# A head's exponentials move behind the first piece of projection work on ScalarE

## The chip, the cores and the metric

One core of a Trainium2 chip. The metric is the device time of one execution in microseconds (us); three runs of the kernel before gave 1851.01, 1851.04 and 1851.13.

## The reference, cut to what matters

Two layers on 256 tokens of width 2048, float32. Layer 0 mixes the tokens with a convolution module, layer 1 with the attention below, and behind each stands a squared-ReLU MLP.

```python
def mla(h, cos, sin, w_in, q_norm_g, kv_norm_g, w_q_up, w_kv_up, w_o):
    down = h @ w_in
    c_q, c_kv, k_pe = jnp.split(down, [512, 1024], axis=-1)
    q = (rms_norm(c_q, q_norm_g) @ w_q_up)        # 16 heads of 128 + 64
    kv = (rms_norm(c_kv, kv_norm_g) @ w_kv_up)    # 16 heads of 128 (k) + 128 (v)
    ...
    s = (q_nope . k_nope + rope(q_pe) . rope(k_pe)) * scale, masked by chunks of 64
    p = softmax(s)
    return (p @ v) @ w_o
```

## The kernel before

Every matmul in full precision is made of three in a rounded format: a value is split into an upper part `hi` and a lower part `lo`, and three products of the parts are summed. For weights the split is made on the fly: ScalarE (ACT) rounds the loaded tile `raw` into `hi` (L174) and VectorE (DVE) subtracts to get `lo` (L175). Results in PSUM that feed another such product are split in the same way (ACT at L224, DVE at L229).

The attention of layer 1 runs 16 heads in 4 groups of 4. The order on each engine is that of the code, since the whole part is written under a manual schedule. Each engine works through its own queue in order and waits at an instruction until its inputs are there. In turn of the loop (L1722 to L1748) for a head `h` stand:

1. `scores(h)`: ten matmuls on TensorE (PE) into one PSUM bank, for the two halves of the queries (128 and 256 keys); DVE takes the maximum of each row (L1582) and scales it by -SCALE (L1583); ACT makes the two exponentials (L1585), which also sum their rows, into `pr`.
2. `piece`: a piece of the work of a later group. It is 12 matmuls of the projections of q or kv (`qp_piece`, `qn_piece`, `kv_piece`), with a copy on ACT or DVE behind them, or from head 12 on 12 wider matmuls of the output projection (`o_piece`), with none. Some pieces also put a delayed copy to `qhl` on ACT (`qp_parts`, L1531), which reads a rotation that GpSimd (POOL) has made at L1322 to L1327.
3. `prefetch(1)`: the split of one half of a weight tile, so one `hi` on ACT and one `lo` on DVE, and behind the second half of a tile the load of another on SP's queue.
4. A second piece.
5. `weights_turn(h - 1)`: PE transposes the previous head's weights `pr` (three transposes, L1601), and ACT copies them to `pT` (L1603).
6. In some heads `qp_turn`: four transposes (L1539) and two copies on ACT (L1548, L1549).
7. `values(h - 2)`: three matmuls (L1610, L1611), split into `oh` and `ol`.
8. `weights(h)`: DVE takes the reciprocal of the sums (L1592) and scales `pr` (L1595). This is what step 5 of the next head waits for.
9. Another split, and up to two more pieces, each with a split.

PSUM has 8 banks for all of this. From head 12 on four of them hold the output projection. The `raw` tiles have 3 buffers, `hi` and `lo` 6 each.

Of the kernel before, what the change touches and what calls it, by code (L numbers as in the profile page):

```python
# [87 lines left out]
def trunk_kernel(  # L88
# [55 lines left out]
    def nm(s):  # L144
        uid[0] += 1
        return f"{s}_{uid[0]}"


    def acc_tile():
        return psum["acc"].tile([P, NB], F32, tag="acc", name=nm("acc"))  # L150
# [56 lines left out]
    def mm3_as_is(ps, sh, sl, mh, ml, start, stop):  # L207

        nc.tensor.matmul(ps, sh, mh, start=start, stop=False)  # L209
        nc.tensor.matmul(ps, sl, mh, start=False, stop=False)  # L210
        nc.tensor.matmul(ps, sh, ml, start=False, stop=stop)  # L211
# [1098 lines left out]
    with ExitStack() as cx:  # L1310
# [61 lines left out]
        def u_load(n):  # L1372
            if n < len(units):
                srcs, shape = units[n]
                raw = raws[n] = wpool.tile(shape, F32, tag="raw", name=nm("raw"), bufs=3)
                for i, src in enumerate(srcs):
                    dst = raw if len(srcs) == 1 else raw[:, i : i + 1, :]
                    if len(src.shape) == 4:
                        dst = dst.rearrange("p j (h n) -> p j h n", h=src.shape[2])
                    nc.sync.dma_start(dst, src)  # L1380

        def u_split(n, h):
            if n < len(units):
                parts[n, h] = split_half(raws[n], h, nc.vector)
# [14 lines left out]
        def prefetch(n=9):  # L1399
            while pending and n > 0:  # L1400
                n -= 1
                u, h = pending.pop(0)
                u_split(u, h)
                if h == 1:
                    u_load(u + 3)
# [114 lines left out]
        def piece(work):  # L1520

            due = list(later)
            work()
            for e in due:
                e[0] -= 1
                if e[0] == 0:
                    later.remove(e)
                    e[1]()
# [5 lines left out]
        def qp_turn(g, m):  # L1534

            pt = tr_tile()
            for i in range(2):
                for t in range(T):
                    nc.tensor.transpose(  # L1539
                        pt[:, i * S + t * P : i * S + (t + 1) * P],  # L1540
                        qps[g, t][:, 2 * m + i, :, :].rearrange("p a b -> p (a b)").bitcast(F32),
                        ident,
                    )
            if m == 0:
                qpAs[g] = gp[0].tile([P, HG, S], F32R, tag="qpA", name=nm("qpA"))
            hs = slice(2 * m, 2 * m + 2)
            o = pt.rearrange("p (i n) -> p i n", i=2)
            nc.scalar.activation(qpAs[g][:, hs, :], o, AF.Copy)  # L1548
            nc.scalar.activation(qpB[g % 2][:DR, hs, :], o[:DR], AF.Copy)  # L1549
# [9 lines left out]
        def group_work(g):  # L1559
            kv = kv_work(g)  # L1560
            return q_work(g) + kv


        sides = [(0, 0, P), (1, P, S)]
        scs, prs, zss, pTs = {}, {}, {}, {}

        def scores(h):

            g, i = divmod(h, HG)
            ss = scs[h] = acc_tile()  # L1570
            mx = at2.tile([P, T], F32, tag="mx", name=nm("mx"))
            zs = zss[h] = at2.tile([P, T], F32, tag="zs", name=nm("zs"))
            pr = prs[h] = at2.tile([P, 3 * P], F32, tag="pr", name=nm("pr"))
            for t, at_, n in sides:
                o = ss[:, at_ : at_ + n]
                ts = slice(t * P, (t + 1) * P)
                qT, kT = ([a[:, i, :] for a in x] for x in (qTs[g], kTs[g]))
                mm3_as_is(o, qT[0][:, ts], qT[1][:, ts], kT[0][:, :n], kT[1][:, :n], True, False)
                nc.tensor.matmul(o, qpAs[g][:, i, ts], kpA[:, :n], start=False, stop=False)
                nc.tensor.matmul(o, qpB[g % 2][:, i, ts], kpB[:, :n], start=False, stop=True)  # L1580
            for t, at_, n in sides:
                nc.vector.tensor_reduce(mx[:, t : t + 1], ss[:, at_ : at_ + n], axis=AX.X, op=ALU.max)  # L1582
            nc.vector.tensor_scalar(mx, mx, scalar1=-SCALE, scalar2=None, op0=ALU.mult)  # L1583
            for t, at_, n in sides:
                nc.scalar.activation(  # L1585
                    pr[:, at_ : at_ + n], ss[:, at_ : at_ + n], AF.Exp, bias=mx[:, t : t + 1], scale=SCALE,
                    accum_out=zs[:, t : t + 1],
                )

        def weights(h):  # L1590
            pr, zs = prs[h], zss.pop(h)
            nc.vector.reciprocal(zs, zs)  # L1592
            for t, at_, n in sides:
                q = pr[:, at_ : at_ + n]
                nc.vector.tensor_scalar(q, q, scalar1=zs[:, t : t + 1], scalar2=None, op0=ALU.mult)  # L1595

        def weights_turn(h):
            pr = prs.pop(h)
            pt = tr_tile()
            for b in range(3):  # L1600
                nc.tensor.transpose(pt[:, b * P : (b + 1) * P], pr[:, b * P : (b + 1) * P], ident)  # L1601
            pT = pTs[h] = gp[0].tile([P, 3 * P], F32, tag="pT", name=nm("pT"))
            nc.scalar.activation(pT, pt[:, : 3 * P], AF.Copy)  # L1603

        def values(h):
            g, i = divmod(h, HG)
            pT = pTs.pop(h)
            vs = slice(i * DV, (i + 1) * DV)
            o = acc_tile()[:, :S]
            nc.tensor.matmul(o, vvs[g][:, 0, vs], pT[:, :S], start=True, stop=False)  # L1610
            nc.tensor.matmul(o[:, P:], vvs[g][:, 1, vs], pT[:, S:], start=False, stop=True)  # L1611
            hi_part(o, oh[:, h, :])
            lo_part(o, oh[:, h, :], ol[:, h, :])
# [6 lines left out]
        def o_piece(k):  # L1620
            m, j = divmod(k, 2)
            if k == 0:
                ps_o.extend([[acc_tile() for _ in range(T)] for _ in range(2)])
            start_unit(("o", m), j)
            wh, wl = w_at(("o", m), j)
            for b in range(2):
                bs = slice(b * NB, (b + 1) * NB)
                for t in range(T):
                    mm3(ps_o[b][t], oh_kt(k, t), ol_kt(k, t), wh[:, bs], wl[:, bs], k == 0, k == H - 1)

        with tc.manual_schedule():
# [90 lines left out]
            for g in range(NG):  # L1722
                for i in range(HG):
                    h = g * HG + i

                    n = -(-len(work) // (HG - i))
                    todo, work = work[:n], work[n:]
                    scores(h)
                    piece(todo.pop(0))
                    prefetch(1)  # L1730
                    piece(todo.pop(0))


                    if h > 0:
                        weights_turn(h - 1)
                    if i > 1 and g + 1 < NG:
                        qp_turn(g + 1, i - 2)
                    if h > 1:
                        values(h - 2)
                    weights(h)  # L1740
                    prefetch(1)
                    for w in todo:
                        piece(w)
                        prefetch(1)
                if g + 2 < NG:
                    work = group_work(g + 2)
                elif g + 2 == NG:
                    work = [lambda k=k: o_piece(k) for k in range(H - HG)]  # L1748
# [94 lines left out]
```

## Time and profile before

| | |
|---|---|
| median of 3 runs | 1851.04 us |
| the profiled execution | 1850.8 us |
| its span | 1849.0 us |
| mean granted TensorE clock | 0.998 |
| HBM traffic over the span | 198 GB/s |
| heads, by the first scores and the last values | about 1023 to 1150 us |

The span is the part of an execution in which the profile has instructions; 1.8 us lie around it. Lines are those of the kernel before. A row of the timeline has its start, its duration, the engine, the line, the operation, output and input tiles with their shapes, and how often it stands in sequence; a bracket tells how long the engine was idle before it and what ended that. PEld is the loading of TensorE's stationary operand, which overlaps matmuls.

### The profile page before, as it was taken

What the parts mean: (1) busy time and instruction counts of PE and PEld (TensorE: products, weight loads), DVE (VectorE), ACT (ScalarE), POOL (GpSimd) and SP (SyncE); (2) the same over time, 40 slices, a digit from 0 to 9 for tenths busy, and PEclk for the clock granted to TensorE, in tenths of its full rate; (3) what the DMA queues carried; (4) which work ended last, traced back from release to release, by engine and by line L of the source; (5) the groups of instructions that cost most, each with busy time, mean ns of one, the idle gap of its engine ahead of it and who ended that gap; (6) DMA issues with size and microseconds to landing.
All of it is one profiled execution on the core that took longest, in us unless ns stands there. A gap on an engine that the chain in (4) does not pass through costs nothing.

```text
span 1849.0 us, 28519 instructions
## 1 busy us (share of the span) xinstructions
PE 1816.2 (98%) x10768; PEld 1655.3 (90%) x10768; DVE 1635.4 (88%) x2370; ACT 1205.5 (65%) x1716; POOL 222.6 (12%) x185
## 2 busy tenths in 40 slices
PE   7999999999999999999999999999999999999998
PEld 6999888988988989898899998899898898899886
DVE  5999975789999999999977675667999999999987
ACT  5556663767667677676566665566766766767654
POOL 5999500000000000000001420000000000000000
PEclk9999999999999999999999999999999999999999
DMA  8766366857667666766546445765766766677673
GB/s 236 198 189 185 123 217 182 217 168 226 201 210 230 196 215 223 227 208 218 204 158 196 125 138 197 208 189 170 217 205 211 231 205 204 219 212 220 212 244 114
DMA packets 407113, 367.62 MB, mean 199 GB/s; under 512 B 15416, under 2 KB 351936, under 8 KB 406720
## 3 DMA queue, kind: packets, MB, share of 16 engines
q1 hardware_dynamic: 405952, 363.63, 64.6%
q10 hardware_dynamic: 1024, 2.17, 0.3%
q8 instruction: 84, 1.38, 0.3%
q14 instruction: 53, 0.43, 0.1%
HBM read 363.68 MB, written 2.10 MB: 198 GB/s over the span
## 4 chain that ended last, share of the span: by engine, by line
PE 81%; DVE 14%; ACT 3%; issue 1%; DMA 1%; POOL 0%; DVEq 0%; ACTq 0%
PE acc L539 23%; PE acc L210 14%; PE acc L209 14%; PE acc L211 14%; PE acc L535 12%; DVE sum L1002 8%; DVE lo L175 1%; DVE lo L444 1%; PE acc L274 1%; ACT hi L174 1%; PE acc L219 0%; PE acc L218 0%; PE acc L220 0%; ACT pr L1585 0%; DMA xs<-in_x 0%
## 5 line engine op out<-in xcount | busy, mean ns | idle before, releaser
L444 DVE TENSOR_TENSOR lo<-raw,hi 128x1024 fp32r<-128x1024 f32 (+1 forms) x512 | 571.3, 1125 | 48.6 <-ACT hi L443 48.4
L443 ACT ACTIVATE hi<-raw 128x1024 fp32r<-128x1024 f32 (+1 forms) x512 | 477.2, 968 | 66.5 <-PE acc L210 62.6
L539 PE MATMUL acc<-xt,hi 128*128 128x512 f32 x2048 | 478.5, 380 | 1.7 <-ACT U L547 1.2
L539 PEld LDWEIGHTS acc<-xt,hi 128*128 128x128 f32 x2048 | 377.8, 190 | 49.8 <-ACT U L547 2.0
L209 PE MATMUL acc<-hi,sh 128*128 128x512 f32 x930 | 353.9, 381 | 0.0
L211 PE MATMUL acc<-lo,sh 128*128 128x512 f32 x930 | 353.0, 380 | 0.0
L210 PE MATMUL acc<-hi,sl 128*128 128x512 f32 x802 | 304.4, 380 | 0.0
L535 PEld LDWEIGHTS acc<-xt,lo 128*128 128x128 f32 x2048 | 249.2, 192 | 7.8 <-DVE lo L444 1.0
L535 PE MATMUL acc<-xt,lo 128*128 128x256 f32 x2048 | 250.5, 276 | 0.4 <-DVE lo L444 0.3
L174 ACT ACTIVATE hi<-raw 128x1024 fp32r<-128x1024 f32 (+2 forms) x184 | 179.6, 1004 | 42.5 <-PE acc L210 39.4
L211 PEld LDWEIGHTS acc<-lo,sh 128*128 128x128 f32 x930 | 176.2, 189 | 24.6
L209 PEld LDWEIGHTS acc<-hi,sh 128*128 128x128 f32 x930 | 176.2, 189 | 24.1
L175 DVE TENSOR_TENSOR lo<-raw,hi 128x1024 fp32r<-128x1024 f32 (+2 forms) x118 | 132.8, 1145 | 62.7 <-ACT hi L174 62.4
L210 PEld LDWEIGHTS acc<-hi,sl 128*128 128x128 f32 x802 | 151.9, 189 | 21.1
L1002 DVE SCALAR_TENSOR_TENSOR sum<-ub,w_dw,sum 128x256 f32<-128x256 f32 x392 | 159.5, 498 | 6.0 <-ACT sum L958 5.0
L443 ACT ACTIVATE hi<-V 128x1024 fp32r<-128x1024 f32 x94 | 99.8, 1062 | 96.2 <-DVE V L749 91.6
L175 POOL TENSOR_TENSOR lo<-raw,hi 128x1024 fp32r<-128x1024 f32 x66 | 156.6, 2385 | 22.7 <-ACT hi L174 20.6
L547 ACT ACTIVATE U<-acc 128x512 f32<-128x512 f32 x128 | 75.6, 591 | 127.5 <-PE acc L539 113.4
L218 PE MATMUL acc<-xt,hi 128*128 128x256 f32 x512 | 142.5, 278 | 0.0
L219 PE MATMUL acc<-xt,hi 128*128 128x256 f32 x512 | 141.2, 276 | 0.7 <-DVE xt L231 0.7
L443 ACT ACTIVATE hi<-T 128x1024 fp32r<-128x1024 f32 x94 | 99.1, 1055 | 65.0 <-DVE T L739 60.6
L220 PE MATMUL acc<-xt,lo 128*128 128x256 f32 x512 | 141.2, 276 | 0.0
(275 smaller groups left out, 2803.3 us busy)
## 6 DMA issues: line engine op xcount, KB each, us to landing
raw<-in_mlp_w SPq DMA_DIRECT2D x256, 1024.0 KB, 6.5
raw<-in_conv_w_pw SPq DMA_DIRECT2D x64, 512.0 KB, 5.6
raw<-in_conv_w_pw SPq DMA_DIRECT2D x16, 1024.0 KB, 5.1
raw<-in_mla_w_o SPq DMA_DIRECT2D x16, 1024.0 KB, 5.6
raw<-in_mla_w_kv_up SPq DMA_DIRECT2D x8, 1024.0 KB, 5.4
raw<-in_mla_w_in SPq DMA_DIRECT2D x8, 576.0 KB, 3.9
raw<-in_mla_w_in SPq DMA_DIRECT2D x4, 1024.0 KB, 6.8
raw<-in_mla_w_q_up SPq DMA_DIRECT2D x16, 256.0 KB, 4.4
```

Of the source, the lines that this page charges most:

```text
L174: nc.scalar.activation(hi, raw[:, js, :], AF.Copy)
L175: eng.tensor_tensor(lo, raw[:, js, :], hi.bitcast(F32), op=ALU.subtract)
L209: nc.tensor.matmul(ps, sh, mh, start=start, stop=False)
L210: nc.tensor.matmul(ps, sl, mh, start=False, stop=False)
L211: nc.tensor.matmul(ps, sh, ml, start=False, stop=stop)
L218: nc.tensor.matmul(ps, wh, alternate(th), start=start, stop=False)
L219: nc.tensor.matmul(ps, wh, alternate(tl), start=False, stop=False)
L443: nc.scalar.activation(parts[0], src, AF.Copy)
L444: nc.vector.tensor_tensor(parts[1], src, parts[0].bitcast(F32), op=ALU.subtract)
L535: nc.tensor.matmul(ps[0][:, :S], wl[:, j, :], alternate(xh(k)), start=False, stop=False)
L539: nc.tensor.matmul(ps[0], wh[:, j, :], xhl(k).rearrange("p (g a b) -> p g b a", g=2, a=2), start=k == 0, stop=k == KC - 1,)
L1002: nc.vector.scalar_tensor_tensor(out=out, in0=ubs[c][:, w : w + S], scalar=tap(c, w), in1=pcs[c], op0=ALU.mult, op1=ALU.add)
```

## The change

`scores(h)` keeps its matmuls, the maximum and its scaling. The two exponentials become a function of their own, `exponentials(h)`, which the loop calls behind the first piece and the split that goes with it, ahead of the second piece.

```diff
@@ scores
             nc.vector.tensor_scalar(mx, mx, scalar1=-SCALE, scalar2=None, op0=ALU.mult)
+            mxs[h] = mx
+
+        def exponentials(h):
+            ss, mx, zs, pr = scs.pop(h), mxs.pop(h), zss[h], prs[h]
             for t, at_, n in sides:
                 nc.scalar.activation(
                     pr[:, at_ : at_ + n], ss[:, at_ : at_ + n], AF.Exp, bias=mx[:, t : t + 1], scale=SCALE,
@@ the loop over heads
                     scores(h)
                     piece(todo.pop(0))
                     prefetch(1)
+                    exponentials(h)
                     piece(todo.pop(0))
```

The order of the instructions on PE, DVE, POOL and SP is the same in both kernels; on ACT the exponentials stand elsewhere. The scores' PSUM bank is given back one step later in the program, so some of the following tiles lie in other banks.

ACT's queue in heads 0 and 1, before. `pr` and `zs` are the exponentials and their sums, `scratch` the copy of a first piece, `hi` the upper parts, `kTh` copies of the second and third piece, `qhl` the copies that read POOL's rotation:

```order
L1585 ACTIVATE pr_10942,zs_10941<-acc_10939,mx_10940 128x128
L1585 ACTIVATE pr_10942,zs_10941<-acc_10939,mx_10940 128x256
L1511 ACTIVATE scratch<-acc_10958 128x256
L174 ACTIVATE hi_10984<-raw_10736 128x1024
L224 ACTIVATE kTh_10990<-acc_10993 128x256
L174 ACTIVATE hi_11011<-raw_10795 128x512
L224 ACTIVATE kTh_10990<-acc_11015 128x256
L224 ACTIVATE qhl_10934<-qp_10923 128x4x64
L1585 ACTIVATE pr_11035,zs_11034<-acc_11032,mx_11033 128x128
L1585 ACTIVATE pr_11035,zs_11034<-acc_11032,mx_11033 128x256
L224 ACTIVATE qhl_10983<-qp_10972 128x4x64
L174 ACTIVATE hi_11067<-raw_10795 128x512
```

The same stretch of ACT's queue with the change (the numbers of tiles differ a little between the two kernels):

```order
L1511 ACTIVATE scratch<-acc_10956 128x256
L174 ACTIVATE hi_10982<-raw_10736 128x1024
L1589 ACTIVATE pr_10942,zs_10941<-acc_10939,mx_10940 128x128
L1589 ACTIVATE pr_10942,zs_10941<-acc_10939,mx_10940 128x256
L224 ACTIVATE kTh_10990<-acc_10993 128x256
L174 ACTIVATE hi_11011<-raw_10795 128x512
L224 ACTIVATE kTh_10990<-acc_11015 128x256
L224 ACTIVATE qhl_10934<-qp_10923 128x4x64
L224 ACTIVATE qhl_10981<-qp_10970 128x4x64
L174 ACTIVATE hi_11065<-raw_10795 128x512
L1589 ACTIVATE pr_11035,zs_11034<-acc_11032,mx_11033 128x128
L1589 ACTIVATE pr_11035,zs_11034<-acc_11032,mx_11033 128x256
```

In head 0 the exponentials moved behind one copy and one upper part, in head 1 behind a `qhl` copy and an upper part.

ACT's queue from the end of head 4 into head 5, before; `qTh` are the copies of the pieces of the next group's queries:

```order
L224 ACTIVATE qhl_11292<-qp_11281 128x4x64
L1585 ACTIVATE pr_11387,zs_11386<-acc_11384,mx_11385 128x128
L1585 ACTIVATE pr_11387,zs_11386<-acc_11384,mx_11385 128x256
L224 ACTIVATE qTh_11346<-acc_11403 128x256
L224 ACTIVATE qhl_11322<-qp_11311 128x4x64
L174 ACTIVATE hi_11420<-raw_11071 128x1024
L224 ACTIVATE qTh_11346<-acc_11426 128x256
```

And with the change:

```order
L224 ACTIVATE qhl_11290<-qp_11279 128x4x64
L224 ACTIVATE qTh_11346<-acc_11401 128x256
L224 ACTIVATE qhl_11322<-qp_11311 128x4x64
L174 ACTIVATE hi_11418<-raw_11069 128x1024
L1589 ACTIVATE pr_11387,zs_11386<-acc_11384,mx_11385 128x128
L1589 ACTIVATE pr_11387,zs_11386<-acc_11384,mx_11385 128x256
L224 ACTIVATE qTh_11346<-acc_11426 128x256
```

Here the exponentials of head 5 moved behind the copy of the first piece, a `qhl` copy and an upper part.

More of the change, by code (lines that the diff above doesn't have):

```diff
@@ L1564, in trunk_kernel @@
         sides = [(0, 0, P), (1, P, S)]
-        scs, prs, zss, pTs = {}, {}, {}, {}
+        scs, prs, zss, pTs, mxs = {}, {}, {}, {}, {}
         def scores(h):
```

## The prediction

> **What bounds the kernel now.** The page comes first, for which engine is full.
>
> ```profile
> span 1849.0 us, 28519 instructions
> PE 1816.2 (98%) x10768; PEld 1655.3 (90%) x10768; DVE 1635.4 (88%) x2370; ACT 1205.5 (65%) x1716; POOL 222.6 (12%) x185
> ```
>
> PE (TensorE) is busy for 98% of the span, so the time can only change by what PE stands idle, and only in the stretch that the change touches: the 16 attention heads. The table by stage for heads 1 to 11 says how much that is. Its columns are the stretch, its length, the busy time of PE, PEld, DVE, ACT and POOL with the number of instructions, the granted clock, and the DMA's share and rate.
>
> ```profile
> 1028.00:1101.00 73.00, 70.43 (x599) 68.67 (x598) 50.32 (x120) 46.28 (x123) 25.40 (x40) 1.00 0.45 136
> ```
>
> Neither DVE (50.32 of 73 us) nor ACT (46.28) is full there, the clock is 1.00, and PE lacks 2.57 us. The waits in the stretch of all 16 heads name what PE, ACT and DVE wait for (total, times, longest):
>
> ```profile
> PE acc L1601 <- DVE pr L1595: 2.3, 4, 1.4
> PE acc L1601 <- ACT kTh L224: 0.3, 1, 0.3
> ```
>
> ```profile
> ACT pr L1585 <- DVE mx L1583: 41.1, 16, 3.7
> ```
>
> ```profile
> DVE lo L175 <- ACT hi L174: 24.6, 17, 2.3
> ```
>
> PE waits five times, always at L1601, where it turns the weights of the head before, which DVE has scaled at L1595. Behind it stands a ring of two engines: ACT cannot start its exponentials (L1585) until DVE has the maximum (L1583), in each of the 16 heads, and then DVE waits for the upper part of the next weights (hi, L174), which ACT could have made long ago but has queued behind the exponentials. Each waits in turn for the other, neither is full, and the ring runs later than PE.
>
> What this costs PE is read from the starts of its rows. First a head in which nothing waits, then the five that wait: in each the last matmul of the second piece, the three transposes, and what follows.
>
> ```profile
> 1065.16 0.28 PE L211 MATMUL acc<-lo,kvh 128*128 128x256 f32 x1
> 1065.27 0.49 PE L1601 MATMUL acc<-ident,pr 128*128 128x128 f32 x3
> 1065.60 0.60 PE L1539 MATMUL acc<-ident,qhl 128*128 128x128 f32 x4
> ```
>
> ```profile
> 1032.32 0.28 PE L211 MATMUL acc<-lo,kvh 128*128 128x256 f32 x1
> 1032.82 0.83 PE L1601 MATMUL acc<-ident,pr 128*128 128x128 f32 x3 [0.23 <-DVE pr L1595]
> 1033.41 0.31 PE L209 MATMUL acc<-kTh,qTh 128*128 128x128 f32 x1
> ...
> 1037.20 0.28 PE L220 MATMUL acc<-kvh,lo 128*128 128x256 f32 x1
> 1038.85 0.61 PE L1601 MATMUL acc<-ident,pr 128*128 128x128 f32 x3 [1.37 <-DVE pr L1595]
> 1039.29 0.60 PE L1539 MATMUL acc<-ident,qhl 128*128 128x128 f32 x4
> ...
> 1044.09 0.27 PE L211 MATMUL acc<-lo,kvh 128*128 128x256 f32 x1
> 1044.77 0.61 PE L1601 MATMUL acc<-ident,pr 128*128 128x128 f32 x3 [0.41 <-DVE pr L1595]
> 1045.22 0.60 PE L1539 MATMUL acc<-ident,qhl 128*128 128x128 f32 x4
> ...
> 1093.37 0.28 PE L211 MATMUL acc<-lo,kvh 128*128 128x256 f32 x1
> 1093.90 0.61 PE L1601 MATMUL acc<-ident,pr 128*128 128x128 f32 x3 [0.26 <-ACT kTh L224]
> 1094.35 0.60 PE L1539 MATMUL acc<-ident,qhl 128*128 128x128 f32 x4
> ...
> 1100.50 0.28 PE L211 MATMUL acc<-lo,kvh 128*128 128x256 f32 x1
> 1101.10 0.61 PE L1601 MATMUL acc<-ident,pr 128*128 128x128 f32 x3 [0.32 <-DVE pr L1595]
> 1101.55 0.60 PE L1539 MATMUL acc<-ident,qhl 128*128 128x128 f32 x4
> ```
>
> Without a wait the transposes start 0.11 us behind the last matmul and take 0.33 until the next row. In the five heads the first distance is 0.50, 1.65, 0.68, 0.53 and 0.60, the second 0.59, 0.44, 0.45, 0.45 and 0.45. The excess of both is 0.65 (head 1), 1.65 (head 2), 0.69 (head 3), 0.54 (head 10) and 0.61 (head 11): **4.1 us** in all.
>
> The idle column of the same rows, with the two waits quoted above, says only 2.6 us. [...] I take the starts, because they are measured against the same rows in a head without a wait.
>
> **The change, part by part.** No instruction is added or removed. The two exponentials of a head, each with its read-out of the sum, go on ACT's queue behind two groups: what the first piece puts there (one copy of 128x256, a copy to qhl too in heads 1, 5 and 9, or nothing), and one upper part. PE, DVE, POOL and SP keep their order, so no DMA is moved past anything.
>
> *Removed: ACT's upper part waiting for the maximum.* The rows of heads 0 and 1, ACT first, then DVE:
>
> ```profile
> 1024.84 1.08 ACT L174 ACTIVATE hi<-raw 128x1024 fp32r<-128x1024 f32 x1
> 1028.15 0.37 ACT L1585 ACTIVATE pr<-acc,mx 128x128 f32<-128x128 f32 x1 [2.23 <-DVE mx L1583]
> ...
> 1029.22 1.07 ACT L174 ACTIVATE hi<-raw 128x1024 fp32r<-128x1024 f32 x1
> ...
> 1035.39 0.37 ACT L1585 ACTIVATE pr<-acc,mx 128x128 f32<-128x128 f32 x1 [3.73 <-DVE mx L1583]
> ...
> 1036.20 0.41 ACT L224 ACTIVATE qhl<-qp 128x256 fp32r<-128x256 f32 x1
> 1036.51 0.62 ACT L174 ACTIVATE hi<-raw 128x512 fp32r<-128x512 f32 x1
> ```
>
> ```profile
> 1027.92 0.19 DVE L1583 TENSOR_SCALAR mx<-mx 128x2 f32<-128x2 f32 x1
> 1030.32 1.54 DVE L175 TENSOR_TENSOR lo<-raw,hi 128x1024 fp32r<-128x1024 f32 x1 [2.20 <-ACT hi L174]
> ...
> 1032.30 0.86 DVE L1595 TENSOR_SCALAR pr<-pr,zs 128x128 f32<-128x128 f32 x2
> ...
> 1035.19 0.17 DVE L1583 TENSOR_SCALAR mx<-mx 128x2 f32<-128x2 f32 x1
> ...
> 1037.16 0.81 DVE L175 TENSOR_TENSOR lo<-raw,hi 128x512 fp32r<-128x512 f32 x1 [1.48 <-ACT hi L174]
> 1037.89 0.41 DVE L1486 COPY vv<-acc 128x256 f32<-128x256 f32 x1
> ...
> 1038.41 0.55 DVE L1595 TENSOR_SCALAR pr<-pr,zs 128x128 f32<-128x128 f32 x2
> ```
>
> Head 0: ACT is free at 1025.92 and idle for 2.23 us. With the change it makes the upper part in that time, and DVE starts the lower part right behind the maximum, at 1028.1 and not at 1030.3: the wait of 2.20 is gone. The exponentials still start at 1028.15; DVE is then in the lower part until 1029.7 and does not miss them. Scaled weights come about 2.2 us earlier, at 1030.1; PE wants them at 1032.43 (0.11 behind 1032.32). Head 1's wait of 0.65 goes.
>
> Head 1: its maximum, behind the same DVE queue, is done at 1035.36 - 2.2 = 1033.2. Here the exponentials are now also behind the qhl copy, which waits for POOL's rotation:
>
> ```profile
> 1030.73 1.44 POOL L1325 TENSOR_TENSOR m<-scratch,sin 128x128 f32<-128x128 f32 x1
> ...
> 1032.55 0.46 POOL L1327 TENSOR_TENSOR qp<-m,m 128x128 f32<-128x128 f32 x1
> ```
>
> *Added: that wait.* POOL is done at 1033.0; then copy (0.3, from 1036.20 to 1036.51) and upper part (0.6) end at 1033.9, the lower part (0.7 to the next row) at 1034.7, the copy of vv at 1035.1. The exponentials start at 1033.9 and take 0.8 with their read-outs (from 1035.39 to 1036.20). The scaling starts at 1035.3, 3.1 us earlier than at 1038.41. PE, relieved of 0.65, wants it at 1037.31 - 0.65 = 1036.66: 1.3 us to spare, and head 2's 1.65 goes.
>
> Head 3 and heads 10 and 11 wait by the same ring, in which each lower part waits 24.6 / 17 = 1.4 us on average; taking the upper part out of the path shortens a head's turn by about that, and their excess is 0.54 to 0.69 each. So these go too. The last four heads have no wait to lose.
>
> *Later exponentials themselves.* They release the scores' PSUM bank later in the queue and delay the second piece's copy by up to 0.8 us when ACT is already waiting for PE. No row of before shows that order. From below, the cost is zero (ACT has 41.1 us of idle time in front of the exponentials); from above, 0.8 us at the scaling of each head, which in head 1 is less than the 1.3 to spare. I take zero, since every head has more spare ACT time than that.
>
> **Sum.** The profiled execution took 1850.8 (span 1849.0 and 1.8 around it); less 4.1 is 1846.7. The median of the runs, 1851.04, is 0.2 above the profiled one, so the forecast is **1846.9**. PE is full behind the heads, and what it gains there moves everything behind it. A difference under 0.2% (3.7 us) counts as none, being about what a measurement of this kernel can tell. The forecast's 4.1 is just above that, so a single leftover wait decides between the two.
>
> **The rivals.**
>
> *One wait stays.* POOL's rotation instructions come in two lengths, 0.46 and 1.44 (the rows above); the long one began at 1030.73, while DVE ran the lower part of 1.54 us from 1030.32. DVE's lower parts move, and three more long ones (3 x 0.98 = 2.9 us) would use up head 1's 1.3 and leave 1.6 at head 2, as large as now: the gain is 4.1 - 1.65 = 2.5 and the time 1848.6. For it: the lower parts stand closer together now. Against it: the rotation has the same instructions, and DVE as many lower parts. [...] Chance 0.28.
>
> *Nothing is won.* DVE itself is late and not the ring: then the upper part arrives earlier, DVE does no more per head, and PE waits as now: 1851.0. Against it stands DVE's busy 50.32 of 73 us. Chance 0.12.
>
> *Slower.* The qhl copy ahead of the exponentials makes POOL the bound of three groups (heads 1, 5 and 9). If all five short instructions of a rotation became long (4.9 us), PE would wait 4.9 - 1.3 = 3.6 in each, 10.8 in all, and the time would be 1851.0 + 10.8 - 4.1 = 1857.7. It is slower from the point where the rotation ends 2.7 us later in all three (1.3 and a third of 4.1). Against it: before shows one long instruction in this rotation. Chance 0.06.
>
> **How the numbers follow.** The forecast has 0.54. Its own range is 1846.2 to 1847.6: 0.7 to either side, about the size of one of the smaller excesses, for gaps that the five places miss or for one that stays; below 1847.3 counts as faster. One stays and nothing won count as no change. The range for 8 in 10 takes in the forecast and most of the first rival: 1846.2 to 1849.2. Faster 0.53, the same 0.41, slower 0.06.
>
> **What would show it.** In the changed profile, the lower part at L175 in head 0 should start right behind the maximum, the wait of DVE for hi in the heads should fall from 24.6 us to under 10, the wait of ACT for the maximum from 41.1 to under 20, and PE's waits for scaled weights should be gone, the transposes at 0.11 behind the last matmul. Wrong would be: a wait at the transposes of head 2 with POOL ahead of the qhl copy (one stays), DVE's waits gone and PE's not (nothing won), or PE waiting for the scores' bank.

## The result and the profile after

| | before | changed |
|---|---|---|
| median of 12 runs each | 1850.95 us | 1846.68 us |
| lowest and highest | 1850.72 to 1851.13 | 1846.44 to 1846.97 |
| the profiled execution, its span | 1850.8, 1849.0 | 1846.85, 1845.1 |
| ratio, 95% interval | | 0.9977 (0.997 to 0.9985) |

The changed kernel is 4.3 us faster; 4.1 was forecast. In all quotes below, lines behind L1584 stand 4 higher than before: the exponentials are L1589, the scaling L1599, the transposes L1605 (kernels with added lines differ by some more).

The page of the changed kernel first, then its table by stage from the scores of head 0 to head 11 (the columns as in the prediction). It is 70 us long here and not 73, because the same work ends earlier:

```profile
span 1845.1 us, 28522 instructions
PE 1814.8 (98%) x10768; PEld 1652.8 (90%) x10768; DVE 1635.3 (89%) x2370; ACT 1206.9 (65%) x1716; POOL 222.9 (12%) x185
```

```profile
1028.00:1098.00 70.00, 70.00 (x610) 69.54 (x609) 53.83 (x128) 47.86 (x127) 26.05 (x40) 1.00 0.51 158
```

PE's busy time over the whole program is nearly what it was (1814.8 against 1816.2) and the span is 3.9 shorter: PE does the same work with fewer holes. In the heads it now has none (70.00 of 70.00).

The waits in the stretch of all heads, the largest of DVE and ACT for each other (total, times, longest); a row of PE is no longer among them:

```profile
DVE ol L229 <- ACT oh L224: 27.1, 14, 4.6
...
ACT pr L1589 <- DVE mx L1583: 11.7, 11, 1.5
DVE lo L175 <- ACT hi L174: 9.7, 11, 1.3
```

ACT's wait for the maximum fell from 41.1 us to 11.7, DVE's for the upper part from 24.6 to 9.7. DVE now waits most for `oh`, which stands ahead of a head's scaling in its queue (1.11 us in head 2, where the scaling starts at 1040.79). That costs PE nothing: the scaled weights are still ready before the transposes want them.

The place with the longest wait before, the transposes in head 2, on PE's timeline:

```profile
1036.79 0.28 PE L220 MATMUL acc<-kvh,lo 128*128 128x256 f32 x1
1036.90 0.49 PE L1605 MATMUL acc<-ident,pr 128*128 128x128 f32 x3
1037.22 0.60 PE L1539 MATMUL acc<-ident,qhl 128*128 128x128 f32 x4
```

The transposes start 0.11 us behind the last matmul and take 0.32, as in a head without a wait; before it was 1.65 and 0.44. No transposes of heads 1 to 11 start later than that now (from head 12 on, behind the wider matmuls, the distance is 0.22 us in both kernels). Measured so, by the starts of the rows, the excess of all heads was 4.25 us before (the five places of the prediction and 0.15 at head 4) and is nothing now.

Heads 0 and 1 on ACT's timeline of the changed kernel:

```profile
1026.76 1.06 ACT L174 ACTIVATE hi<-raw 128x1024 fp32r<-128x1024 f32 x1
1028.45 0.37 ACT L1589 ACTIVATE pr<-acc,mx 128x128 f32<-128x128 f32 x1 [0.63 <-DVE mx L1583]
...
1033.73 0.42 ACT L224 ACTIVATE qhl<-qp 128x256 fp32r<-128x256 f32 x1 [2.58 <-POOL qp L1327]
1034.05 0.62 ACT L174 ACTIVATE hi<-raw 128x512 fp32r<-128x512 f32 x1
1034.57 0.35 ACT L1589 ACTIVATE pr<-acc,mx 128x128 f32<-128x128 f32 x1
```

And on DVE's:

```profile
1028.22 0.19 DVE L1583 TENSOR_SCALAR mx<-mx 128x2 f32<-128x2 f32 x1
1028.33 1.21 DVE L175 TENSOR_TENSOR lo<-raw,hi 128x1024 fp32r<-128x1024 f32 x1
...
1030.20 1.06 DVE L1599 TENSOR_SCALAR pr<-pr,zs 128x128 f32<-128x128 f32 x2
...
1033.03 0.28 DVE L1583 TENSOR_SCALAR mx<-mx 128x2 f32<-128x2 f32 x1
...
1034.70 0.93 DVE L175 TENSOR_TENSOR lo<-raw,hi 128x512 fp32r<-128x512 f32 x1 [1.07 <-ACT hi L174]
...
1036.08 0.55 DVE L1599 TENSOR_SCALAR pr<-pr,zs 128x128 f32<-128x128 f32 x2
```

In head 0 the upper part is made while DVE still works on the maximum, the lower part starts 0.11 us behind the start of the maximum's scaling (L1583), and the exponentials run beside it. The scaling of the weights starts at 1030.20 where it stood at 1032.30. In head 1 the exponentials do stand behind the `qhl` copy, which waits 2.58 us for POOL; the scaling ends at 1036.63 and the transposes start at 1036.90. That is 0.27 us to spare, the least of all 16 heads. (This execution came to its heads about 0.3 us later than the one before: its maximum ends at 1028.41, the other's at 1028.11. So its span is 3.9 us shorter, where the excess fell by 4.25.)

POOL's second rotation on its timeline:

```profile
1028.36 1.51 POOL L1325 TENSOR_TENSOR m<-scratch,sin 128x128 f32<-128x128 f32 x1
...
1031.55 0.90 POOL L1324 TENSOR_TENSOR m<-scratch,cos 128x128 f32<-128x128 f32 x1
...
1033.24 0.46 POOL L1327 TENSOR_TENSOR qp<-m,m 128x128 f32<-128x128 f32 x1
```

It ends at 1033.70, and at 1033.01 before. The long instructions lie elsewhere: one of 1.51 over DVE's lower part at 1028.33, one of 0.90 over that at 1031.19; the 1.44 at 1030.73 is gone.

### The profile page after: what moved, and what is told of

It reads as the page before. It is cut to its first block, busy times and chain, and to the rows that moved or that the text cites. A ratio compares the mean times of both kernels' runs of the same rounds, so it can differ in the third digit from the quotient of the medians.

```text
span 1845.1 us, 28522 instructions
## 1 busy us (share of the span) xinstructions
PE 1814.8 (98%) x10768; PEld 1652.8 (90%) x10768; DVE 1635.3 (89%) x2370; ACT 1206.9 (65%) x1716; POOL 222.9 (12%) x185
## 3 DMA queue, kind: packets, MB, share of 16 engines
q10 hardware_dynamic: 1024, 2.17, 0.3%
## 4 chain that ended last, share of the span: by engine, by line
PE 86%; DVE 10%; issue 1%; ACT 1%; DMA 1%; SPq 0%; DVEq 0%; POOL 0%; ACTq 0%
PE acc L539 23%; PE acc L210 15%; PE acc L209 15%; PE acc L211 15%; PE acc L535 12%; DVE sum L1002 7%; PE acc L219 1%; PE acc L218 1%; PE acc L220 1%; DVE lo L444 1%; PE acc L274 1%; DMA xs<-in_x 0%; PE acc L1614 0%; DVE T L739 0%; DMA pos_i<-in_positions 0%
## 5 line engine op out<-in xcount | busy, mean ns | idle before, releaser
L209 PEld LDWEIGHTS acc<-hi,sh 128*128 128x128 f32 x930 | 175.8, 189 | 24.6
L175 DVE TENSOR_TENSOR lo<-raw,hi 128x1024 fp32r<-128x1024 f32 (+2 forms) x118 | 132.3, 1141 | 46.7 <-ACT hi L174 46.4
L175 POOL TENSOR_TENSOR lo<-raw,hi 128x1024 fp32r<-128x1024 f32 x66 | 156.4, 2383 | 22.7 <-ACT hi L174 20.5
```

The source lines that it names most:

```text
L175: eng.tensor_tensor(lo, raw[:, js, :], hi.bitcast(F32), op=ALU.subtract)
```

## The experiments

The theory: the gain comes from the upper part alone, which no longer stands in ACT's queue behind the wait for the maximum; the transposes' waits in heads 1, 2, 3, 10 and 11 go by it, and POOL's rotation has room in head 1. Rivals: another thing that moves with it does it (the copies, or the PSUM banks that the tiles get); the waits at heads 10 and 11 are not costs of those heads, but a delay carried there from the first; the exponentials' later place costs something that the gain hides; POOL is nearer to the path than forecast.

The ten kernels of the experiments were timed in three comparisons of five rounds, each beside the kernel before (medians of 1850.72, 1850.81 and 1850.89), from which the gain is taken; the changed kernel stands with its own. "Left" is the excess that remains at the transposes, by the starts of the rows, where the wait at the transposes is what the kernel tells.

| kernel | median us | ratio (95%) | gain us | left us |
|---|---|---|---|---|
| changed | 1846.68 | 0.9977 (0.997 to 0.9985) | 4.27 | 0 |
| copy first | 1848.56 | 0.9988 (0.9979 to 0.9996) | 2.33 | 2.0 |
| upper part only | 1846.45 | 0.9976 (0.9967 to 0.9985) | 4.44 | 0 |
| last | 1846.35 | 0.9976 (0.9967 to 0.9985) | 4.46 | 0 |
| first four heads | 1846.57 | 0.9977 (0.9967 to 0.9986) | 4.32 | 0 |
| last twelve heads | 1849.94 | 0.9995 (0.9986 to 1.0004) | 0.95 | 3.4 |
| head 0 alone | 1848.47 | 0.9988 (0.9979 to 0.9997) | 2.25 | 2.0 |
| long rotation | 1852.91 | 1.0013 (1.0004 to 1.0022) | -2.10 | |
| the same, exponentials ahead | 1851.50 | 1.0005 (0.9996 to 1.0014) | -0.69 | |
| long rotation in the heads | 1851.12 | 1.0 (0.9991 to 1.0009) | -0.40 | 3.2 |
| the same, exponentials ahead | 1848.22 | 0.9987 (0.9978 to 0.9996) | 2.50 | |

Gain and left add up to 4.2 to 4.5 us in the first seven rows: the starts of PE's rows tell the time within about 0.2 us.

### Which part of the move does it

**Copy first.** The exponentials stand behind the first piece's copy, but ahead of the upper part. Against the changed kernel:

```diff
                     piece(todo.pop(0))
-                    prefetch(1)
                     exponentials(h)
+                    prefetch(1)
                     piece(todo.pop(0))
```

> The exponentials stand behind the first piece only and ahead of its upper part, so the upper part waits for the maximum again, while the first piece's copy and the PSUM banks are as in the changed kernel. Theory (the ring is DVE waiting for an upper part that stands behind the exponentials): most of the gain is lost, DVE's wait for hi in the heads is back over 18 us, PE waits at the transposes again, 1848.0 to 1850.5 us. Rival 1 (what matters is the first piece's copy, or the other PSUM banks): 1846.7, no wait of PE.

Measured: 1848.56 us. The waits among ACT and DVE in the heads, then head 2 on PE's timeline, both of this kernel:

```profile
ACT pr L1589 <- DVE mx L1583: 29.1, 16, 2.8
DVE lo L175 <- ACT hi L174: 27.6, 18, 2.0
```

```profile
1036.57 0.28 PE L220 MATMUL acc<-kvh,lo 128*128 128x256 f32 x1
1037.75 0.61 PE L1605 MATMUL acc<-ident,pr 128*128 128x128 f32 x3 [0.91 <-DVE pr L1599]
1038.20 0.60 PE L1539 MATMUL acc<-ident,qhl 128*128 128x128 f32 x4
```

The mutual wait is back (27.6 us of DVE for the upper part, 24.6 before), and the transposes of head 2 start 1.18 us behind the last matmul. So the upper part matters: DVE's order and the PSUM banks are those of the changed kernel, and 1.9 us of its gain are gone. But 2.3 of 4.3 us stay won, with nothing moved except the copy and the `qhl` copy: taking these out from behind the wait also wins time, which the prediction did not cost. (The banks, which change with them, are not tested apart. Against them: before the change PE waits in the heads only at the transposes, and never at the first matmul of a piece.) DVE's total wait for the upper part is thus no measure of the gain: it is above that of before here, with half of the gain won.

**Upper part only.** The copies stay behind the exponentials; only the upper and the lower part go ahead. The functions of the pieces call what is put into `between` behind their matmuls, ahead of their own copy (these calls are not shown):

```diff
+                    between.append(lambda: (prefetch(1), exponentials(h)))
                     piece(todo.pop(0))
-                    prefetch(1)
-                    exponentials(h)
                     piece(todo.pop(0))
```

> Only the upper part (and DVE's lower part) goes ahead of the exponentials; the first piece's copy, and a qhl copy with it, stay behind them. Theory: the whole gain, no wait of PE at the transposes, 1846.4 to 1847.1 us. Rival 1 (the copy or the banks matter): about 1851.

Measured: 1846.45 us, no wait of PE, and DVE hardly waits for the upper part any more:

```profile
DVE lo L175 <- ACT hi L174: 4.1, 6, 1.3
```

Without the copies' move the whole gain comes. It is not ACT's order alone that differs here: in seven heads DVE's lower part also goes ahead of DVE's own copy or lower part of the piece. The transposes of head 2 have 1.12 us to spare, against 0.27 in the changed kernel, since these exponentials do not stand behind the `qhl` copy. The parts do not add up (2.3 by the copies, 4.4 by the upper part, 4.3 by both). The account that fits is that each only has to bring DVE's scaling ahead of PE's need, and that what it brings beyond is worth nothing.

**Last.** The exponentials go as far back as they can, directly ahead of the reciprocal and scaling that read them:

```diff
                     prefetch(1)
-                    exponentials(h)
                     piece(todo.pop(0))
                     ...
+                    exponentials(h)
                     weights(h)
```

> The exponentials go as far back as they can: behind the second piece, the turned weights and the values, just ahead of the scaling that needs them. Theory (they cost nothing where they stand, as long as the upper part is ahead of them and ACT has the time; head 1 has 0.27 us to spare in the changed kernel and loses about that): 1846.6 to 1847.4 us. Rival 3 (each step back delays the scaling of every head by the 0.8 us of the exponentials): waits of PE at heads 2 and 3, 1847.8 to 1849.

Measured: 1846.35 us, 0.25 under what was expected and the lowest median of all, but only 0.33 us under the changed kernel's, and timed beside other runs of the kernel before: not told apart. The place where the exponentials are read, in head 2, on ACT's timeline and then DVE's:

```profile
1038.54 0.37 ACT L224 ACTIVATE oh<-acc 128x256 fp32r<-128x256 f32 x1
1038.81 0.36 ACT L1589 ACTIVATE pr<-acc,mx 128x128 f32<-128x128 f32 x1
```

```profile
1039.74 0.17 DVE L1596 RECIPROCAL zs<-zs 128x2 f32<-128x2 f32 x1 [0.37 <-ACT pr L1589]
1039.94 0.55 DVE L1599 TENSOR_SCALAR pr<-pr,zs 128x128 f32<-128x128 f32 x2
```

The exponentials have no bracket: ACT does not wait for the maximum here. DVE waits for the exponentials instead, 0.37 us. PE does not wait. A later place of the exponentials costs nothing here; at the transposes of head 2 0.29 us are to spare, as in the changed kernel.

### Which heads are worth it

**First four heads, last twelve heads, head 0 alone.** The exponentials stand behind the upper part in some heads and directly behind the scores, as before, in the others. For the first four (`HG` is 4); the other two have the conditions `h < HG` and `h >= HG`, and `h > 0` and `h == 0`, in the two places:

```diff
                     scores(h)
+                    if h >= HG:
+                        exponentials(h)
                     piece(todo.pop(0))
                     prefetch(1)
-                    exponentials(h)
+                    if h < HG:
+                        exponentials(h)
```

> The change in heads 0 to 3 alone, the old order from head 4 on. Theory (each stretch has a ring of its own): PE's excess of 0.54 and 0.61 us at heads 10 and 11 stays, that of heads 1 to 4 goes, 1847.5 to 1848.2 us. Rival 2 (a backlog from the start of the heads is carried through): all waits go, 1846.7.

Measured: 1846.57 us, the whole gain. The transposes in head 11, where PE lost 0.61 us before and where the order is the old one, on DVE's timeline and then PE's:

```profile
1096.01 0.55 DVE L1599 TENSOR_SCALAR pr<-pr,zs 128x128 f32<-128x128 f32 x2
```

```profile
1096.89 0.28 PE L211 MATMUL acc<-lo,kvh 128*128 128x256 f32 x1
1097.01 0.49 PE L1605 MATMUL acc<-ident,pr 128*128 128x128 f32 x3
1097.33 0.60 PE L1539 MATMUL acc<-ident,qhl 128*128 128x128 f32 x4
```

The scaling ends at 1096.56, 0.45 us ahead of the transposes; no PE wait is left. The spare time (from the end of the scaling to the transposes) in heads 5 to 11 is 3.31, 1.68, 2.04, 2.44, 2.69, 1.05 and 0.45 us. Before it is 1.72, 0.06, 0.42, 0.84 and 1.10 in heads 5 to 9, and in heads 10 and 11 PE waits 0.54 and 0.61. The 1.10 of head 9, on the timelines before:

```profile
1084.00 0.87 DVE L1595 TENSOR_SCALAR pr<-pr,zs 128x128 f32<-128x128 f32 x2
...
1085.97 0.49 PE L1601 MATMUL acc<-ident,pr 128*128 128x128 f32 x3
```

The difference is 1.6 us in each of heads 5 to 9: the lead that the first four heads gain is carried through the old order as it is, neither growing nor used up. The old order has its own ups and downs on top of it. From head 9 to head 10 it loses 1.64 us (2.69 to 1.05), to head 11 another 0.60; before, these losses made the waits of 0.54 and 0.61, and here the lead of 1.6 pays for them and 0.45 is left. So the time that the theory gave is wrong and rival 2's is right; but what is carried is the lead, while the delay arises in heads 9 and 10.

> The change in heads 4 to 15 alone, the old order in heads 0 to 3. Theory: the 3.1 us of heads 1 to 4 stay, the 1.15 us of heads 10 and 11 go, 1849.5 to 1850.1 us, and the gains of this run and of the run with the first four heads add up to the whole. Rival 2 (carried backlog): nothing at all, about 1851.

Measured: 1849.94 us, as expected, so rival 2 fails here: the change in the later heads removes their waits too. The waits at heads 1, 2 and 3 are as before (0.66, 1.65, 0.67), that at head 4 grows from 0.15 to 0.41, those at 10 and 11 are gone:

```profile
PE acc L1605 <- DVE pr L1599: 2.0, 3, 1.4
```

The first four heads alone win 4.32 us, the last twelve 0.95, together 5.27, and the whole change 4.27: against the expectation the two do not add up to the whole. The 1.15 us at heads 10 and 11 is counted in both, since either removes it: the later heads by their own order, the first four by their lead.

> The change in head 0 alone, the old order in the 15 others. Theory as it stands after the runs with four and with twelve heads (a backlog is built up by the old order a little in each head and carried): the waits at heads 1 and 2 go (2.3 us), 1.0 to 1.9 us stay at heads 3, 4 or later, 1847.7 to 1848.6 us. Rival 5 (the backlog comes from ahead of the heads, and one head's advance clears it): 1846.5 to 1847.0. Rival 6 (each head's wait is its own): 1850.4, head 1's 0.65 us alone.

Measured: 1848.47 us. Heads 1 and 2 have no excess, head 3 has 0.66, heads 4, 10 and 11 together 1.33. Head 3 on PE's timeline:

```profile
1041.96 0.28 PE L211 MATMUL acc<-lo,kvh 128*128 128x256 f32 x1
1042.62 0.61 PE L1605 MATMUL acc<-ident,pr 128*128 128x128 f32 x3 [0.38 <-DVE pr L1599]
```

One head's lead of 2.2 us (its scaling starts at 1030.09, before at 1032.30) carries over to the next head, in the old order, and removes 1.65 us there too; then it is used up (the scaling of head 1 ends 0.03 us behind the start of the transposes), the waits of heads 3, 10 and 11 are those of before, and the gain ends at 2.25.

### How near POOL's rotation is

**Long rotation.** The changed kernel with three repeats of one multiplication in each of POOL's rotations, which write the same values again; in the second kernel the exponentials also stand ahead of the `qhl` copy, behind the first piece's matmuls, its own copy and the upper part (`piece` calls the function that it is given there):

```diff
@@ rope
+            for _ in range(3 if eng is nc.gpsimd else 0):
+                eng.tensor_tensor(m[3], a, sb, op=ALU.mult)
@@ the loop over heads, in the second kernel
-                    piece(todo.pop(0))
-                    prefetch(1)
-                    exponentials(h)
+                    piece(todo.pop(0), lambda: (prefetch(1), exponentials(h)))
```

> The changed order, with three more multiplications of 128x128 in each of POOL's rotations (they write the same product again). Theory (the qhl copy ahead of head 1's exponentials makes them wait for POOL): the second rotation ends some 2.5 us later, 0.27 us is to spare, PE waits 1.5 to 2.7 us at the transposes of head 2, none in heads 6 and 10 (3.3 us to spare), 1848.1 to 1849.5 us. Rival 4 (POOL is not in the path): 1846.7.

> The same longer rotations, with the exponentials behind the first piece's copy and the upper part, but ahead of the qhl copy that waits for POOL. Theory: no wait at the transposes of head 2; up to 0.8 us may appear at the next transposes (the qhl parts, later now): 1846.5 to 1847.6 us. Rival 4 (a longer rotation costs by itself, by contention with DVE): as much as the run with the longer rotation alone.

Measured: 1852.91 and 1851.50 us, both far over what was expected. The edit was too wide: it also lengthens the rotations of group 0, ahead of the first head, and PE waits for those some 2.2 us in either kernel; in the second, at a granted clock of 0.50 behind that wait (below), it also took 1.6 us longer from the first transpose to the scores of head 0 (1021.49 to 1027.30, 5.81 us, against 1021.80 to 1025.98, 4.18 us). Nor do the runs of one kernel agree: of the first, seven stand at 1852.6 to 1853.0 and four, the traced one among them, at 1854.0 to 1854.3; of the second, nine at 1851.2 to 1851.65, the traced one among them, and two at 1852.97 and 1853.05. The two medians differ by 1.4 us in the sense that the theory gives (the transposes of head 2 have an excess of 3.75 us in the first and 0.08 in the second), but the common part makes them a poor measure. So the edit was made again, for the rotations in the heads only.

**Long rotation in the heads.** Both kernels as above, with the repeats for the groups behind group 0 only (`rope` takes their number as its last argument):

```diff
-            rope(qp, qr, t, HG, nc.gpsimd)
+            rope(qp, qr, t, HG, nc.gpsimd, 3 if g > 0 else 0)
```

> The changed order with the three more multiplications in the rotations of groups 1 to 3 alone, so that the rotation ahead of the heads is as in the changed kernel. Theory (head 1's exponentials wait behind the qhl copy for POOL): PE waits about 3.7 us at the transposes of head 2, as in the run with all rotations longer, nothing ahead of the heads, 1849.9 to 1850.9 us. Rival 4 (that run was slower for what lies ahead of the heads): 1846.7 to 1847.5.

> The same rotations as in the run before, with the exponentials ahead of the qhl copy and behind the upper part. Theory: no wait at the transposes of head 2, about 0.7 us at the next transposes of the rotated queries, 1847.0 to 1848.0 us, so 2 to 3.5 us faster than with the qhl copy ahead. Rival 4 (a longer rotation costs by itself): the same as the run before.

Measured: 1851.12 and 1848.22 us, 2.9 us apart. Of the first, ACT's timeline in head 1, and PE's at the transposes behind it:

```profile
1036.63 0.42 ACT L224 ACTIVATE qhl<-qp 128x256 fp32r<-128x256 f32 x1 [3.68 <-POOL qp L1329]
...
1037.47 0.35 ACT L1591 ACTIVATE pr<-acc,mx 128x128 f32<-128x128 f32 x1
```

```profile
1036.55 0.28 PE L220 MATMUL acc<-kvh,lo 128*128 128x256 f32 x1
1039.38 0.88 PE L1607 MATMUL acc<-ident,pr 128*128 128x128 f32 x3 [2.56 <-DVE pr L1601]
1040.05 1.06 PE L1541 MATMUL acc<-ident,qhl 128*128 128x128 f32 x4
```

The `qhl` copy starts 2.9 us later than in the changed kernel (1036.63 against 1033.73), though this execution comes to the transposes of head 1 0.26 us earlier (1032.48 against 1032.74). That is 3.16 us against PE, and the transposes start 2.72 us late: about what exceeds the 0.27 to spare. The exponentials stand behind POOL, and PE behind the exponentials. In the second kernel they do not, and the transposes are on time:

```profile
1036.68 0.49 PE L1609 MATMUL acc<-ident,pr 128*128 128x128 f32 x3
1037.93 0.33 PE L1543 MATMUL acc<-ident,qhl 128*128 128x128 f32 x1 [0.76 <-POOL qhl L1536]
1038.62 0.55 PE L1543 MATMUL acc<-ident,qhl 128*128 128x128 f32 x3 [0.36 <-POOL qhl L1536]
```

What remains there are waits for the rotated queries themselves, which stand behind the rotation in either order. The `qhl` copies of heads 5 and 9 are behind longer rotations too, and cost next to nothing: the changed kernel has 3.35 us to spare in both heads. In the first kernel that is just used up (0.05 left in head 6, an excess of 0.12 in head 10), in the second 0.8 is left in each. The first time is 0.2 over what was expected, and the second too; of the first, the granted clock of 0.50 behind its wait tells why (below).

## Why the prediction was right, and where not

*What bounds it: right.* PE's waits at five transposes were worth the 4.1 us read from the starts of the rows. The idle column's 2.6 us would have given 1848.4 (1851.04 less 2.6); the time is 1846.68. A sixth place, head 4, had 0.15 us more and was missed.

*The upper part out of the ring: right.* Shown by the kernel that moves the upper part, and the lower part with it, but no copy (4.4 us), and by the one that moves all but it (nearly half the gain gone). Head 0 came out as forecast: the lower part right behind the maximum, the scaling 2.1 us earlier by the two traces' times and 2.4 counted from the maximum (forecast 2.2). DVE's wait for the upper part is 9.7 (under 10), ACT's for the maximum 11.7 (under 20). The step left out that the copies behind the wait count as well: moved alone, they bring 2.3 us. And small waits between ACT and DVE, its signs, are not needed for the gain: with the order of before from head 4 on, ACT's wait is still 32.7 us and DVE's 21.2, and the whole gain is there.

*Head 1, with 1.3 us to spare: right that its wait goes, wrong in size.* 0.27 us is left. Two things were off. The step compared the start of the scaling with PE's need, and the scaling's own 0.55 us should have been taken off: 0.8 remains. And it put POOL's end at 1033.0, where it was before; it came at 1033.70, 0.4 more than the later heads explain, since instructions of 1.51 and 0.90 stand over DVE's lower parts at their new places, where one of 1.44 stood before. That leaves 0.4, and small shifts make it 0.27. It is the mechanism of the rival *one wait stays*, with 0.4 us in place of the 2.9 that it took, and 0.3 us more would have begun to bring its wait: a rotation prolonged by about 2.9 us did.

*Heads 3, 10 and 11 "wait by the same ring", "so these go too": right, but not the only way.* With the new order from head 4 on alone, the waits of heads 10 and 11 go, as the step says. With the new order in the first four heads alone they go too, by the lead of 1.6 us that is carried to them; that the step did not foresee. Nor is a shorter turn of a head a gain of fixed size: the lead of one head serves the next ones until their losses use it up (head 0 alone).

*Later exponentials at no cost: right.* Moved further back still, they cost nothing (1846.35).

*The rival* slower*: its place is right and its price is not.* It gave all three heads the 1.3 us to spare of head 1; head 1 has 0.27, heads 5 and 9 have 3.35. With the rotations some 3 us longer the time came back to the kernel before's, about where the rival puts that point (2.7 us in each head). That agreement is luck: it was one wait of 2.7 us and a clock of 0.50 in the 2.8 us behind it (below), and not three waits. *Nothing is won* fell with the waits: PE's went with DVE's.

Not settled: whether the last 0.2 to 0.3 us between the changed kernel and those with the upper part only or with the exponentials last is real, and how much of the copies' 2.3 us is theirs and not the banks'.

## What to carry to other kernels

Where two engines that work in order wait for each other in turn and neither is full, look for an instruction whose inputs are long there, queued behind one that waits: put it ahead, and the waiting instruction as late as its reader allows. Price such waits on TensorE by the distance of row starts against the same rows where nothing waits, and ask of each wait whether a lead gained in earlier stages would cover it, since a change there can then remove it as well. Before an instruction is put behind a wait for a third engine, take the work of its readers off the time to spare, and look whether that engine's instructions become longer where another engine's work moves over them, as POOL's did here (0.90 and 1.51 us in place of 0.46).

## What the runs showed of the hardware

**Behind a wait of 2.5 us TensorE's granted clock was 0.50; behind waits of 1.50 and 0.35 us it was 0.50 in one run and 1.00 in another.** The table of the kernel with the long rotation in the heads, at its wait (the last three columns are the granted clock, the DMA's share and its rate):

```profile
1036.80:1039.30 2.50, 0.03 (x1) 0.00 (x0) 1.67 (x5) 2.50 (x9) 1.16 (x2) 0.94 0.00 0
1039.30:1042.10 2.80, 2.72 (x12) 2.55 (x12) 2.69 (x7) 2.44 (x8) 0.00 (x0) 0.50 0.86 257
```

Of the kernel before, around its longest wait:

```profile
1037.30:1038.90 1.60, 0.23 (x3) 0.09 (x1) 1.56 (x6) 0.21 (x1) 0.12 (x1) 1.00 0.00 0
1038.90:1042.00 3.10, 3.10 (x26) 2.99 (x27) 1.23 (x6) 2.21 (x7) 0.00 (x0) 1.00 0.92 276
```

Behind 2.5 us without matmuls the clock is 0.50 through the next 2.8 us; behind 1.4 us it stays 1.00. From the transposes of head 2 to those of head 3 PE takes 6.75 us there (1039.38 to 1046.13) and 5.25 in the changed kernel (1036.90 to 1042.15): 1.5 us more, with no wait of PE in it. With the 2.72 that the transposes start late that is 4.2, and from the transposes of head 1 to the last ones this trace takes 4.24 us longer than the changed kernel's (111.13 against 106.89). So this wait cost half as much again.

At the wait ahead of the heads, the first and then the second of the kernels with long rotations everywhere:

```profile
1020.00:1022.00 2.00, 0.51 (x4) 0.25 (x2) 0.00 (x0) 0.89 (x2) 2.00 (x5) 1.00 0.92 206
1022.00:1024.00 2.00, 1.65 (x15) 1.52 (x15) 0.42 (x1) 1.99 (x4) 0.42 (x1) 1.00 0.01 1
1024.00:1026.00 2.00, 2.00 (x21) 2.00 (x20) 1.72 (x3) 2.00 (x6) 0.00 (x0) 1.00 0.00 0
```

```profile
1020.00:1022.00 2.00, 0.33 (x1) 0.14 (x1) 0.00 (x0) 1.19 (x2) 2.00 (x4) 1.00 0.83 186
1022.00:1024.00 2.00, 1.83 (x12) 1.83 (x13) 0.45 (x2) 1.99 (x5) 0.12 (x1) 0.71 0.00 0
1024.00:1026.00 2.00, 2.00 (x11) 2.00 (x11) 1.86 (x3) 2.00 (x6) 0.00 (x0) 0.50 0.00 0
```

PE is idle for 1.84 us of these first four in both, 1.50 and 0.35 with one transpose of 0.33 between, and the clock falls to 0.50 in one and stays in the other: in 1024 to 1026 PE starts 21 matmuls in the first kernel and 11 in the second. So the same gap came out both ways; why is not shown. That probably also tells why 2 of the 11 runs of the kernel with the long rotation in the heads stand at 1849.6 to 1849.7, with a mean granted clock of 0.999, and the others at 1851.0 to 1851.25, with 0.997 or 0.998. Whether it also tells why the kernels with long rotations everywhere have two groups is open: their mean clocks, 0.997 to 0.999, do not part the groups. No kernel has a trace of both of its groups, so neither is shown.

**POOL's instructions took longer over DVE's lower parts.** From 1000 to 1150 us in the traces before and after, the 128x128 instruction of POOL's rotation took 0.45 to 0.47 us where DVE had no lower part of weights (L175), and up to 1.51 over one, as at 1028.36 (1.51) and 1031.55 (0.90) in the changed kernel: the long ones have more lengths than the prediction's one of 1.44, and they moved with the lower parts from one kernel to the other. Not each one that meets a lower part is long: before the change, the one at 1030.32 took 0.46 while DVE's lower part began beside it, and the next one 1.44. What makes them longer is not shown.
